# Folded weight chunks whose accumulating transfer begins ahead of their cast, transposes one step later, and one folded pair more in each down block

## The chip, the core and the metric

The kernel runs on one core of a Trainium2 chip. The time is the device time of one execution in microseconds (us), as the median of several executions. Beside it there is one profiled execution, from which all views of the trace come; its time is a little above the median of the others.

## The reference

One decoder layer in float32, with 256 tokens (`x` is 1 x 256 x 2048): a first feed-forward block, two token mixers side by side (retention and sliding-window attention), a second feed-forward block and a gated per-layer embedding, each followed by a layer norm. The two feed-forward blocks take most of the time, and the change lies in them:

```python
D_MODEL, SEQ, D_FF = 2048, 256, 5632
def swiglu(x, w_gu, w_down):
    g, u = jnp.split(x @ w_gu, 2, axis=-1)
    return (jax.nn.silu(g) * u) @ w_down
...
h = layer_norm(alpha * h + 0.5 * swiglu(h, w_ffn1_gu[i], w_ffn1_down[i]), ln_g[i, 0], ln_b[i, 0])
...
h = layer_norm(alpha * h + mixed, ln_g[i, 1], ln_b[i, 1])
h = layer_norm(alpha * h + 0.5 * swiglu(h, w_ffn2_gu[i], w_ffn2_down[i]), ln_g[i, 2], ln_b[i, 2])
```

## The kernel before

**Products in three matmuls.** The matmuls run on fp32r data. A float32 operand is split in a high part (a rounding copy on ACT, line 105) and a low part (the rest, a subtraction on DVE, line 106), and a product is three matmuls: low by high, high by high, high by low (`Sum.add`, lines 431 to 433). The activations are the stationary operand, the weights move: each matmul is 128 x 128 by 128 x 512.

**Chunks and slots.** Weights come from memory in chunks of 128 x 1024 words (512 KB), by transfers on SP's queue (line 119 and its neighbours: `Chunk`). A chunk's raw, high and low form take one slot each of a pool of 46 slots (`SLOTS`), which the weights share with other buffers; `slots_for_weights(n)` says how many of them the weights may use from that point on.

**Units.** The rows of a weight matrix are taken in pairs of 128-row blocks, and the columns in two halves. A pair is one unit of a block's order string: `P` is plain, two `Single` chunks of 12 matmuls each. `S` is a `Seven`: four quarter products by seven multiplications instead of eight (21 matmuls instead of 24), for which DVE first adds raw quarters to each other (lines 226 to 229) and two more forms, u and v, are split. `D` is a `Seven` of the second feed-forward block whose forms were prepared ahead of it and are only loaded. `F` is *folded*: a `Single`, and then a `Folded` chunk, whose low part DVE does not make. ACT writes minus the raw data, rounded (line 169), POOL issues a transfer inside the chip's memory that adds the raw data to it (line 170), and ACT makes the high part by a rounding copy (line 171).

**Two matrices.** In the first feed-forward block (names with f1) the gate and up products run in 11 groups `j` of 512 columns each: group 0 is all `P`, the others have the order "FFSSFSSP" (three `F`, four `S`, one `P`). In the second (f2), groups 1 to 3 have no `F`, groups 4 to 7 one, group 8 two, 9 and 10 three. After a group's last `S`, `seven_common` combines the sums (lines 549 to 553: one copy on ACT, then additions on DVE into tiles `eve` and `evw`), the Silu follows on ACT (line 1057), and the result is transposed: a `Turn` copies halves of words on ACT (line 185), SP moves them by a transposing transfer (line 189), ACT joins them again (line 196). The down product has two halves of the columns, with the orders FIRST_DOWN and SECOND_DOWN over 22 pairs; the tile names are f1d, f1e (or f2d, f2e) for its sums.

**What sets the order.** The program text is generated in the order in which the engines run it, and `plan` is a list of units in the order of use. `fill` moves units on: it loads the next of the plan while fewer than `far` matmuls' worth of units are waiting and slots are left, and it lets ACT, DVE and POOL make the next loaded unit while less than `ahead` (45) matmuls' worth of them is ready. Each unit says how many slots its load takes (`loads`), how many its making needs (`makes`) and how many it holds until its use (`keeps`), and its matmuls (`time`). `take` gives the next ready unit to PE, `done` frees its slots and calls `fill`. After each unit `run_side` does one waiting side job: `later(n, job)` puts a job n steps on. A transpose is such a job: its transfer is issued DELAY steps after its copies, and the join three steps after that (`turned`, lines 984 to 995). SP's, POOL's and each engine's instructions run in order: one that waits holds all behind it.

Of the kernel before, what the change touches and what calls it, by code (L numbers as in the profile page):

```python
# [9 lines left out]
F32R = mybir.dt.float32r  # L10
# [28 lines left out]
SLOTS = 46  # L39


SEVEN = (0, 1, 2, 3)

AHEAD = {1: (4, 5), 2: (4,), 3: (4, 5), 4: (4,), 5: (4, 5), 6: (4,), 7: (4, 5)}
AHEAD_SLOTS = 36

DELAY = 1

SEVEN_DOWN = (6, 7, 8, 9)

FIRST_DOWN = "PPPPPPFFSFSPSFSPSFSSPS"
SECOND_DOWN = "PPPSPSPSFSPSFSSPSPPPPP"
LEAD = 4

# [8 lines left out]
def layer(ctx: ExitStack, tc: tile.TileContext, io):  # L63
# [16 lines left out]
    def slot(shape, dt, name):  # L80
        return slots.tile(shape, dt, tag="slot", name=name)
# [6 lines left out]
    plan = []  # L88
# [19 lines left out]
    class Chunk:  # L108
# [31 lines left out]
    class Single:  # L140


        loads, makes, keeps, time = 1, 2, 2, 12
# [4 lines left out]
        def load(self, **how):  # L148
            self.chunk = Chunk(self.key, **how)
# [1 line left out]
        def make(self):  # L151
            self.chunk.make()

    class Folded:

        loads, makes, keeps, time = 1, 2, 2, 12

        def __init__(self, key):  # L160
            self.key = key

        def load(self, **how):
            self.chunk = Chunk(self.key, **how)

        def make(self):
            c = self.chunk
            c.make_hi()
            act.mul(c.lo, c.raw, -1.0)
            pool.dma_start(c.lo, c.raw, accum_op=ALU.add)  # L170
            act.copy(c.hi, c.raw)

    class Turn:

# [138 lines left out]
    loaded, ready = [], []  # L313
    room = {"slots": 0, "used": 0, "ahead": 45, "far": 90, "quiet": False}

    def fill(must=False):

        while True:
            queued = sum(u.time for u in ready)
            left = room["slots"] - room["used"]  # L320
            wanted = must and not ready or not room["quiet"] and queued < room["ahead"]
            if loaded and wanted and loaded[0].makes <= left:
                u = loaded.pop(0)
                u.make()
                room["used"] += u.keeps - u.loads
                ready.append(u)
                continue
            first = loaded[0] if loaded else plan[0] if plan else None
            queued += sum(u.time for u in loaded)
            if plan and queued < room["far"] and plan[0].loads + first.makes <= left:  # L330
                u = plan.pop(0)
                u.load()
                room["used"] += u.loads
                loaded.append(u)
                continue
            return

    def make_next():
        u = loaded.pop(0)
        assert u.makes <= room["slots"] - room["used"]  # L340
        u.make()
        room["used"] += u.keeps - u.loads
        ready.append(u)

    def take(key):
        if not ready:
            fill(True)
        u = ready.pop(0)
        assert u.key == key, (u.key, key)
        return u  # L350
# [5 lines left out]
    def slots_for_weights(n, ahead=45, far=90):  # L356
        room.update(slots=n, ahead=ahead, far=far)
# [95 lines left out]
    def block_units(units, keys):  # L453

        for kind, p in units:
            if kind == "P":
                plan.extend(Single(keys(n, p)) for n in range(2))
            elif kind == "F":
                plan.extend(of(keys(n, p)) for n, of in enumerate((Single, Folded)))
            else:  # L460
                plan.append((Seven if kind == "S" else Prepared)(keys(0, p), keys(1, p)))

# [511 lines left out]
    def ffn(name, i, ht, norm, keep, residual, keepers, away):  # L974
# [33 lines left out]
        for j in range(KF // 4):  # L1008
            pg, pu = banks(f"{name}g{j}"), banks(f"{name}u{j}")
            units = gu_units(name, j)  # L1010
            n_of = {(0, 0): KD, (0, 1): KD, (1, 0): KD, (1, 1): KD}
            for kind, p in units:
                if kind in "SD":
                    for at in ((0, 0), (0, 1), (1, 0)):
                        n_of[at] -= 1
                    n_of[1, 1] -= 2
            sums = [[Sum((pg, pu)[n][t], n_of[t, n]) for n in range(2)] for t in range(2)]
            got = []

            if norm is not None and j == 0:  # L1020
                front, units = units[:FRONT_PAIRS], units[FRONT_PAIRS:]
                steps = [(gu_keys(name, 0)(n, p), 2 * p, n) for _, p in front for n in range(2)]
                norm.by_transfer = 3,
                norm.first(steps, rhs, sums, (
                    (3, (1, 0)), (5, "more"), (5, (1, 1)), (7, (0, 2)), (8, (1, 2)), (9, (0, 3)), (9, (1, 3)),
                    (10, ("move", 3)), (10, "go"),
                ))
                later(1, lambda: norm.join(3))
                slots_for_weights(24)

            def before(u, j=j, offset=KD // 2 - len(units)):
                u += offset
                if j == 0 and norm is None and u % 2 == 0:
                    first_chunk(u // 2)
                    if u == 6:
                        slots_for_weights(24)
                    if u == 2:
                        load_constants()
                if j == 0 and u == 7:
                    for g in sorted({p // 2 for p in SEVEN}):  # L1040
                        hi, lo = (slot([P, 8, P], F32R, f"{name}f{w}{g}") for w in "hl")
                        made[g] = seven_forms(keep[g], hi, lo)
                    if name == "f2":
                        g = AHEAD[1][0] // 2
                        made[g] = forms_of([ht[:, 4 * g : 4 * g + 4, :]], f"{name}f{g}")
                if name == "f2" and j and u == 0:
                    slots_for_weights(AHEAD_SLOTS - j)
                if j == KF // 4 - 1 and u in (4, 6):
                    convert(u // 2 - 2)

            block(f"{name}{j}", units, gu_keys(name, j), rhs, forms, sums, lambda *a: got.extend(seven_common(*a)), before)
            if got:
                g, v = got
                for x, ps in ((g, pg), (v, pu)):
                    for t in range(2):
                        dve.tensor_tensor(x[:, t], x[:, t], ps[t], ALU.add)  # L1056
                act.activation(g, g, AF.Silu)  # L1057
                dve.tensor_tensor(v, g, v, ALU.mult)
            else:
                v = slot([P, 2, 512], F32, f"{name}v{j}")  # L1060
                for t in range(2):
                    act.activation(v[:, t], pg[t], AF.Silu)
                for t in range(2):
                    dve.tensor_tensor(v[:, t], v[:, t], pu[t], ALU.mult)
            later(1, lambda j=j, v=v: turned(j, v))
# [878 lines left out]
```

## Time and profile before

| what | us |
|---|---|
| time, median of 3 runs (2226.49 to 2227.42) | 2227.09 |
| the profiled execution's own time | 2230.62 |
| its span in the trace | 2228.6 |
| busy: PE / DVE / ACT / POOL | 2218.5 / 2004.0 / 1439.0 / 50.9 |
| gate and up of the first block, groups 1 to 10 | about 49 to 458 |
| its down product, first and second half | about 458 to 581, 581 to 689 |
| mixers, and the start of the second block | about 689 to 1495 |
| gate and up of the second block, groups 1 to 10 | about 1495 to 1895 |
| its down product, first half | about 1895 to 2018 |

The clock that TensorE was granted is 0.999 of full speed over the span. In the rows of the timeline the first figure is the start in us from the span's start, the second the duration, then engine, line, operation, output<-inputs, and in brackets the idle time of the engine just before and what ended it. Matmuls are pipelined: a row shows 0.39 us for one, while the next begins 0.23 us after it.

### The profile page before, as it was taken

How to read it: one execution, taken by the hardware profiler on the slowest of the kernel's cores; microseconds unless marked ns; L12 is line 12 of the kernel's file. 1: busy time of each engine (PE TensorE's matmuls, PEld its weight loads, DVE VectorE, ACT ScalarE, POOL GpSimd, SP SyncE). 2: the span in 40 equal slices, each digit the busy share in tenths (PEclk: the TensorE clock that was granted, in tenths of full speed). 3: DMA queues.
4: the chain of work that ended last, by engine and by line, in shares of the span. 5: the costliest groups of instructions: out<-in, count | busy, mean ns of one | idle time of the engine just before them, and what ended most of it. 6: DMA issues, size and time to landing. Idle time of an engine off the chain costs nothing.

```text
span 2228.6 us, 29103 instructions
## 1 busy us (share of the span) xinstructions
PE 2218.5 (100%) x10140; PEld 1838.9 (83%) x10140; DVE 2004.0 (90%) x2624; ACT 1439.0 (65%) x1677; POOL 50.9 (2%) x65
## 2 busy tenths in 40 slices
PE   9999999999999999999999999999999999999998
PEld 8888888888888888888788888888888888888887
DVE  6999999989998789789999888779999999999977
ACT  6777777777565545557865567466766677765653
POOL 0000000000000000000000000000000000000000
PEclk9999999999999999999999999999999999999999
DMA  9988998976686889757976568888999999666871
GB/s 321 250 264 252 249 263 241 269 227 217 228 305 234 298 283 338 203 179 232 291 233 226 184 203 321 316 302 266 301 301 295 300 248 276 209 233 221 309 283 68
DMA packets 302075, 570.51 MB, mean 256 GB/s; under 512 B 98652, under 2 KB 103388, under 8 KB 301928
## 3 DMA queue, kind: packets, MB, share of 16 engines
q1 hardware_dynamic: 291880, 536.71, 72.3%
q0 software_dynamic: 8064, 29.36, 7.0%
q10 hardware_dynamic: 1984, 2.58, 0.4%
q8 instruction: 79, 1.29, 0.2%
q14 instruction: 68, 0.56, 0.1%
HBM read 487.32 MB, written 31.46 MB: 233 GB/s over the span
## 4 chain that ended last, share of the span: by engine, by line
PE 93%; DMA 3%; DVE 2%; issue 1%; ACT 0%; SPq 0%; ACTq 0%; POOL 0%; DVEq 0%; POOLq 0%
PE rqk L382 3%; PE f2g L431 3%; PE f2g L433 3%; PE f2g L432 3%; PE f1g L431 2%; PE f1g L433 2%; PE f1g L432 2%; PE f2u L431 2%; PE f2u L433 2%; PE f2u L432 2%; PE f1u L433 2%; PE f1u L431 2%; PE f1u L432 2%; PE aqk L382 2%; PE f2e L431 1%; PE f1e L431 1%
## 5 line engine op out<-in xcount | busy, mean ns | idle before, releaser
L106 DVE TENSOR_TENSOR lf_gu<-rf_gu,hf_gu 128x1024 fp32r<-128x1024 f32 (+1 forms) x225 | 267.7, 1210 | 22.1 <-ACT hf_gu L105 21.1
L105 ACT CAST hf_gu<-rf_gu 128x1024 fp32r<-128x1024 f32 (+1 forms) x225 | 228.7, 1039 | 22.1 <-DMA rf_gu<-in_f_gu 21.5
L106 DVE TENSOR_TENSOR lw_in_f<-rw_in_f,hw_in_f 128x1024 fp32r<-128x1024 f32 x140 | 167.8, 1219 | 15.0 <-ACT hw_in_f L105 15.0
L106 DVE TENSOR_TENSOR lf_down<-rf_down,hf_down 128x1024 fp32r<-128x1024 f32 x130 | 155.7, 1220 | 12.9 <-ACT hf_down L105 11.1
L105 ACT CAST huf_gu<-uf_gu 128x1024 fp32r<-128x1024 f32 x76 | 80.1, 1053 | 125.4 <-DVE uf_gu L227 109.4
L105 ACT CAST hf_down<-rf_down 128x1024 fp32r<-128x1024 f32 x130 | 132.7, 1049 | 30.5 <-DMA rf_down<-in_f_down 21.3
L105 ACT CAST hw_in_f<-rw_in_f 128x1024 fp32r<-128x1024 f32 x140 | 140.4, 1049 | 2.3 <-PE gt L433 1.6
L105 ACT CAST hvf_gu<-vf_gu 128x1024 fp32r<-128x1024 f32 x76 | 80.1, 1054 | 32.4 <-DVE vf_gu L229 30.5
L106 DVE TENSOR_TENSOR luf_gu<-uf_gu,huf_gu 128x1024 fp32r<-128x1024 f32 x76 | 92.6, 1218 | 0.0
L106 DVE TENSOR_TENSOR lvf_gu<-vf_gu,hvf_gu 128x1024 fp32r<-128x1024 f32 x76 | 92.6, 1218 | 0.0
L431 PE MATMUL f1g<-hf_gu,xt 128*128 128x512 f32 x232 | 90.8, 391 | 0.0
L433 PE MATMUL f1g<-lf_gu,xt 128*128 128x512 f32 x232 | 90.5, 390 | 0.0
L432 PE MATMUL f1g<-hf_gu,xt 128*128 128x512 f32 x232 | 90.5, 390 | 0.0
L431 PE MATMUL f2g<-hf_gu,ht 128*128 128x512 f32 x211 | 82.2, 390 | 0.0
L433 PE MATMUL f2g<-lf_gu,ht 128*128 128x512 f32 x211 | 82.1, 389 | 0.0
L432 PE MATMUL f2g<-hf_gu,ht 128*128 128x512 f32 x211 | 82.1, 389 | 0.0
L433 PE MATMUL f1u<-lf_gu,xt 128*128 128x512 f32 x192 | 75.0, 391 | 1.2 <-DMA lf_gu<-rf_gu 1.2
L431 PE MATMUL f1u<-hf_gu,xt 128*128 128x512 f32 x192 | 74.7, 389 | 0.0
L432 PE MATMUL f1u<-hf_gu,xt 128*128 128x512 f32 x192 | 74.7, 389 | 0.0
L170 POOL DMA_DIRECT2D lf_gu<-rf_gu x42 | 36.4, 867 | 1641.2 <-DMA rf_gu<-in_f_gu 1017.6
L105 ACT CAST huf_down<-uf_down 128x1024 fp32r<-128x1024 f32 x32 | 33.7, 1054 | 60.7 <-DVE uf_down L227 58.7
L1057 ACT ACTIVATE eve<-eve 128x1024 f32<-128x1024 f32 x20 | 21.2, 1061 | 67.3 <-DVE eve L1056 67.3
(1512 smaller groups left out, 6978.3 us busy)
## 6 DMA issues: line engine op xcount, KB each, us to landing
rf_gu<-in_f_gu SPq DMA_DIRECT2D x361, 512.0 KB
rf_down<-in_f_down SPq DMA_DIRECT2D x176, 512.0 KB
rw_in_f<-in_w_in_f SPq DMA_DIRECT2D x148, 512.0 KB
lf_gu<-rf_gu POOLq DMA_DIRECT2D x42, 512.0 KB, 8.2
rw_rv<-in_w_rv SPq DMA_DIRECT2D x32, 512.0 KB
rw_ret<-in_w_ret SPq DMA_DIRECT2D x32, 512.0 KB
rw_mix<-in_w_mix SPq DMA_DIRECT2D x32, 512.0 KB
rw_pg<-in_w_pg SPq DMA_DIRECT2D x32, 512.0 KB
```

The source lines that it names most:

```text
L105: act.copy(dst_hi, src)
L106: (lo_engine or dve).tensor_tensor(dst_lo, src, dst_hi, ALU.subtract)
L170: pool.dma_start(c.lo, c.raw, accum_op=ALU.add)
L382: pe.matmul(ps[f], hi[:, kk, f * P : (f + 1) * P], rhs(k), start=k == 0, stop=k == n_k - 1,)
L431: pe.matmul(o, al, bh, start=first, stop=False)
L432: pe.matmul(o, ah, bh, start=False, stop=False)
L433: pe.matmul(o, ah, bl, start=False, stop=self.left == 0)
L1057: act.activation(g, g, AF.Silu)
```

## The change

Four edits. **First**, a folded chunk becomes two entries of the plan. `Folding` loads the raw data, and its making is the multiplication on ACT and POOL's accumulating transfer; it has no matmuls (`time` 0) and never comes to `ready`. `Folded` stands where it stood, loads nothing and makes the high part alone. `fold_at` puts the `Folding` 34 matmuls' worth of units ahead (12 in the down product), and if a `Seven` stands within the entries just before that place, ahead of that `Seven`. `take` calls `fill` until something is ready. **Second**, DELAY is 2 instead of 1: a transpose's transfer and its join come one side step later. **Third**, FIRST_DOWN has one `F` more and one `P` less, and its last two adjoining `S` are apart. **Fourth**, in group 0 of the first block the weights get 30 slots instead of 24 from the seventh unit on. The matmuls are the same in number and kind.

```diff
+FOLD_AHEAD = 12, 34
...
-DELAY = 1
+DELAY = 2
...
-FIRST_DOWN = "PPPPPPFFSFSPSFSPSFSSPS"
+FIRST_DOWN = "PPPPPFFSFSFSPSFSPSFSPS"
...
-    class Folded:
-        loads, makes, keeps, time = 1, 2, 2, 12
+    class Folding:
+        loads, makes, keeps, time = 1, 1, 2, 0
...
-        def load(self, **how):
-            self.chunk = Chunk(self.key, **how)
+        def load(self):
+            self.chunk = Chunk(self.key)

         def make(self):
             c = self.chunk
-            c.make_hi()
+            c.lo = slot(list(c.raw.shape), F32R, "l" + c.name)
             act.mul(c.lo, c.raw, -1.0)
             pool.dma_start(c.lo, c.raw, accum_op=ALU.add)
+
+    class Folded:
+        loads, makes, keeps, time = 0, 1, 2, 12
...
+        def make(self):
+            c = self.chunk = self.begun.chunk
+            c.hi = slot(list(c.raw.shape), F32R, "h" + c.name)
             act.copy(c.hi, c.raw)
+            room["used"] -= self.begun.keeps
+
+    def fold_at(ahead, key):
+        begun = Folding(key)
+        at, time = len(plan), 0
+        while at > 0 and time < ahead:
+            at -= 1
+            time += plan[at].time
+        if ahead and any(isinstance(u, Seven) for u in plan[at - 12 : at + 1]):
+            while not isinstance(plan[at], Seven):
+                at -= 1
+        plan.insert(at, begun)
+        plan.append(Folded(begun))
...
-        ready.append(u)
+        if u.time:
+            ready.append(u)
...
-        if not ready:
+        while not ready:
             fill(True)
...
-                plan.extend(of(keys(n, p)) for n, of in enumerate((Single, Folded)))
+                plan.append(Single(keys(0, p)))
+                fold_at(FOLD_AHEAD[keys(1, p)[0][-3:] == "_gu"], keys(1, p))
...
-                        slots_for_weights(24)
+                        slots_for_weights(30)
```

What moves is shown at three places. In the names r, h, l stand for raw, high and low, u and v (with h and l before them) for the two forms of a `Seven` and b for its fourth operand; the two numbers behind gu are the half of the columns and the pair, the last is a running number; the new lines are numbered some 2 (casts) to 30 higher.

ACT in the first block, from the second-last `S` of group 4 (pair 2) on, first before:

```order
L105 CAST huf_gu_0_2_1759<-uf_gu_0_2_1746 128x1024
L105 CAST hvf_gu_0_2_1763<-vf_gu_0_2_1747 128x1024
L105 CAST hf_gu_0_3_1787<-rf_gu_0_3_1691 128x1024
L105 CAST bf_gu_0_3_1791<-rf_gu_1_3_1693 128x512
L105 CAST huf_gu_0_3_1794<-uf_gu_0_3_1781 128x1024
L105 CAST hvf_gu_0_3_1798<-vf_gu_0_3_1782 128x1024
L196 COPY f1a_1804<-mf_1695 128x2x4x128 x2
L105 CAST hf_gu_0_7_1819<-rf_gu_0_7_1723 128x1024
L105 CAST hf_gu_1_7_1846<-rf_gu_1_7_1767 128x1024
L105 CAST hf_gu_0_4_1875<-rf_gu_0_4_1802 128x1024
L169 ACTIVATE lf_gu_1_4_1880<-rf_gu_1_4_1823 128x1024
L171 CAST hf_gu_1_4_1879<-rf_gu_1_4_1823 128x1024
```

and now:

```order
L107 CAST huf_gu_0_2_1763<-uf_gu_0_2_1750 128x1024
L107 CAST hvf_gu_0_2_1767<-vf_gu_0_2_1751 128x1024
L170 ACTIVATE lf_gu_1_4_1785<-rf_gu_1_4_1694 128x1024
L170 ACTIVATE lf_gu_1_5_1788<-rf_gu_1_5_1696 128x1024
L107 CAST hf_gu_0_3_1797<-rf_gu_0_3_1698 128x1024
L107 CAST bf_gu_0_3_1801<-rf_gu_1_3_1700 128x512
L107 CAST huf_gu_0_3_1804<-uf_gu_0_3_1791 128x1024
L107 CAST hvf_gu_0_3_1808<-vf_gu_0_3_1792 128x1024
L107 CAST hf_gu_0_7_1826<-rf_gu_0_7_1725 128x1024
L226 COPY f1a_1830<-mf_1727 128x2x4x128 x2
L107 CAST hf_gu_1_7_1854<-rf_gu_1_7_1771 128x1024
L107 CAST hf_gu_0_4_1881<-rf_gu_0_4_1812 128x1024
```

The multiplications of the next group's folded chunks 4 and 5 stand ahead of the last `S` (pair 3) instead of behind it, with the high part's cast left at its place, and the join `f1a` comes one cast later.

ACT at the end of the same group, from the Silu on, before:

```order
L1057 ACTIVATE eve<-eve 128x1024
L105 CAST hf_gu_0_0_1964<-rf_gu_0_0_1884 128x1024
L105 CAST bf_gu_0_0_1968<-rf_gu_1_0_1886 128x512
L105 CAST huf_gu_0_0_1971<-uf_gu_0_0_1958 128x1024
L105 CAST hvf_gu_0_0_1975<-vf_gu_0_0_1959 128x1024
L185 COPY wf_1995<-evw 128x1024 x2
L105 CAST hf_gu_0_1_2016<-rf_gu_0_1_1911 128x1024
L105 CAST bf_gu_0_1_2020<-rf_gu_1_1_1913 128x512
L105 CAST huf_gu_0_1_2023<-uf_gu_0_1_2010 128x1024
L105 CAST hvf_gu_0_1_2027<-vf_gu_0_1_2011 128x1024
L105 CAST hf_gu_0_6_2047<-rf_gu_0_6_1979 128x1024
L169 ACTIVATE lf_gu_1_6_2079<-rf_gu_1_6_1993 128x1024
```

and now:

```order
L1086 ACTIVATE eve<-eve 128x1024
L170 ACTIVATE lf_gu_1_6_1960<-rf_gu_1_6_1887 128x1024
L107 CAST hf_gu_0_0_1969<-rf_gu_0_0_1889 128x1024
L107 CAST bf_gu_0_0_1973<-rf_gu_1_0_1891 128x512
L107 CAST huf_gu_0_0_1976<-uf_gu_0_0_1963 128x1024
L107 CAST hvf_gu_0_0_1980<-vf_gu_0_0_1964 128x1024
L215 COPY wf_1998<-evw 128x1024 x2
```

Chunk 6's multiplication follows the Silu directly instead of standing eleven rows behind it.

SP's queue at the end of the first half of the down product, with the last pairs' raw chunks, before:

```order
L119 DMA rf_down_20_4717<-in_f_down 128x1024
L119 DMA rf_down_20_4777<-in_f_down 128x1024
L119 DMA rf_down_17_4779<-in_f_down 128x1024
L119 DMA rf_down_17_4781<-in_f_down 128x1024
L119 DMA rf_down_18_4803<-in_f_down 128x1024
L119 DMA rf_down_18_4805<-in_f_down 128x1024
L119 DMA rf_down_21_4911<-in_f_down 128x1024
L119 DMA rf_down_21_4938<-in_f_down 128x1024
L119 DMA rf_down_19_4965<-in_f_down 128x1024
L119 DMA rf_down_19_4967<-in_f_down 128x1024
L119 DMA rf_down_0_4990<-in_f_down 128x1024
L119 DMA rf_down_0_4992<-in_f_down 128x1024
```

and now:

```order
L121 DMA rf_down_20_4740<-in_f_down 128x1024
L121 DMA rf_down_17_4742<-in_f_down 128x1024
L121 DMA rf_down_17_4744<-in_f_down 128x1024
L121 DMA rf_down_20_4766<-in_f_down 128x1024
L121 DMA rf_down_18_4833<-in_f_down 128x1024
L121 DMA rf_down_18_4835<-in_f_down 128x1024
L121 DMA rf_down_21_4853<-in_f_down 128x1024
L121 DMA rf_down_21_4911<-in_f_down 128x1024
L121 DMA rf_down_19_4913<-in_f_down 128x1024
L121 DMA rf_down_19_4915<-in_f_down 128x1024
L121 DMA rf_down_0_4933<-in_f_down 128x1024
L121 DMA rf_down_0_4993<-in_f_down 128x1024
```

The rows stand in nearly the same order on this queue, but they wait for slots that other units free: the matmul that frees a slot for pair 19's second chunk stands 18 places earlier among PE's matmuls than before, in both feed-forward blocks, and the first use of pair 19 stands at the same place.

More of the change, by code (lines that the diff above doesn't have):

```diff
@@ L152, in make, with __init__, load @@
             self.chunk.make()
-    class Folded:
-        loads, makes, keeps, time = 1, 2, 2, 12
+    class Folding:
+        loads, makes, keeps, time = 1, 1, 2, 0
         def __init__(self, key):
             self.key = key
-        def load(self, **how):
-            self.chunk = Chunk(self.key, **how)
+        def load(self):
+            self.chunk = Chunk(self.key)
         def make(self):
             c = self.chunk
-            c.make_hi()
+            c.lo = slot(list(c.raw.shape), F32R, "l" + c.name)
             act.mul(c.lo, c.raw, -1.0)
             pool.dma_start(c.lo, c.raw, accum_op=ALU.add)
-            act.copy(c.hi, c.raw)
+    class Folded:
+        loads, makes, keeps, time = 0, 1, 2, 12
+        def __init__(self, begun):
+            self.key, self.begun = begun.key, begun
+        def load(self):
+            pass
+        def make(self):
+            c = self.chunk = self.begun.chunk
+            c.hi = slot(list(c.raw.shape), F32R, "h" + c.name)
+            act.copy(c.hi, c.raw)
+            room["used"] -= self.begun.keeps
[10 more added lines that the diff above has]
+        plan.append(Folded(begun))
     class Turn:
@@ L322, in fill @@
             if loaded and wanted and loaded[0].makes <= left:
-                u = loaded.pop(0)
-                u.make()
-                room["used"] += u.keeps - u.loads
-                ready.append(u)
+                make_next()
                 continue
@@ L342, in make_next @@
         room["used"] += u.keeps - u.loads
-        ready.append(u)
+        if u.time:
+            ready.append(u)
     def take(key):
-        if not ready:
+        while not ready:
             fill(True)
```

## The prediction

> **What bounds the kernel now.** I read the busy table of the page first, then the waits of PE, then the timeline of PE around each wait, then the engines that released it.
>
> ```profile
> PE 2218.5 (100%) x10140; PEld 1838.9 (83%) x10140; DVE 2004.0 (90%) x2624; ACT 1439.0 (65%) x1677; POOL 50.9 (2%) x65
> ```
>
> PE is busy for 2218.5 of 2228.6 us. The change leaves the matmuls as they are, so it can only alter the time in which PE stands still. The waits of PE say how little that is (engine, line, releaser: total, times, longest):
>
> ```profile
> PE warm L1822 <- POOL ident masks.py:199: 1.4, 1, 1.4
> PE f1u L433 <- DMA lf_gu<-rf_gu: 1.2, 2, 0.9
> PE f1e L431 <- DVE evw L550: 0.6, 1, 0.6
> PE mr1a L433 <- DVE lw_ret L106: 0.5, 1, 0.5
> PE f2e L431 <- DVE evw L550: 0.5, 1, 0.5
> ...
> PE mr1s L433 <- DVE lvw_ret L106: 0.2, 1, 0.2
> ```
>
> The change speaks to the second, third and fifth row. The first is the start, the others lie in the mixers. These figures are too small, because a matmul's shown end (0.39 us after its start) overlaps the next start. The true loss is read from start to start. In steady work starts are 0.2267 us apart; around the waits of f1u:
>
> ```profile
> 74.70 0.50 PE L433 MATMUL f1u<-lf_gu,xt 128*128 128x512 f32 x1 [0.88 <-DMA lf_gu<-rf_gu]
> ...
> 237.81 0.39 PE L432 MATMUL f1u<-hf_gu,xt 128*128 128x512 f32 x1
> 238.54 0.50 PE L433 MATMUL f1u<-lf_gu,xt 128*128 128x512 f32 x1 [0.34 <-DMA lf_gu<-rf_gu]
> 238.88 0.39 PE L431 MATMUL f1u<-hf_gu,xt 128*128 128x512 f32 x1
> ...
> 401.65 0.39 PE L432 MATMUL f1u<-hf_gu,xt 128*128 128x512 f32 x1
> 401.96 0.50 PE L433 MATMUL f1u<-lf_gu,xt 128*128 128x512 f32 x1
> ```
>
> At 238.54 the start is 0.73 us after the one before, 0.50 more than the step, and the next is 0.34 later, 0.11 more than the step: 0.61 us lost where the row says 0.34 idle, so 0.27 is to be added to an idle figure. At 74.70 that makes 0.88 + 0.27 = 1.15. At 401.96 no idle is shown, yet 0.31 − 0.23 + 0.11 = 0.19 is lost. **Together 1.95 us for f1u.**
>
> **Why f1u waits.** The low part of a folded chunk is a multiplication by −1 on ACT (L169) and an accumulating transfer issued by POOL (L170):
>
> ```profile
> 62.38 1.06 ACT L169 ACTIVATE lf_gu<-rf_gu 128x1024 fp32r<-128x1024 f32 x1
> ...
> 63.73 0.86 POOL L170 DMA_DIRECT2D lf_gu<-rf_gu  x1 [15.21 <-ACT lf_gu L169]
> ...
> lf_gu<-rf_gu POOLq DMA_DIRECT2D x1, 512.0 KB, 10.9
> ...
> 228.02 1.06 ACT L169 ACTIVATE lf_gu<-rf_gu 128x1024 fp32r<-128x1024 f32 x1
> ...
> 229.58 0.86 POOL L170 DMA_DIRECT2D lf_gu<-rf_gu  x1 [17.85 <-ACT lf_gu L169]
> ...
> q0 software_dynamic: 144, 0.52, 22.0%
> ...
> lf_gu<-rf_gu POOLq DMA_DIRECT2D x1, 512.0 KB, 8.9
> ```
>
> The last figures of the two "POOLq" rows are the us from issue to landing, from the DMA view of 62 to 75 and of 228 to 240; the q0 row is from the latter. 63.73 + 10.9 = 74.63 and 229.58 + 8.9 = 238.48: in both cases PE goes 0.06 to 0.07 us after the landing. From the start of the multiplication to the landing it is 12.25 and 10.46 us, the longest such stretches I found, and both belong to the third folded chunk of a group (chunk 6).
>
> **Part 1, the earlier accumulation.** In a group of f1 chunk 6's multiplication now follows the Silu (L1057 in the old numbering) directly, and those of chunks 4 and 5 stand ahead of the last seven's first cast. Old rows at these two places, and the first uses of the low parts that the second place serves:
>
> ```profile
> 214.14 1.06 ACT L1057 ACTIVATE eve<-eve 128x1024 f32<-128x1024 f32 x1 [2.69 <-DVE eve L1056]
> 215.11 1.04 ACT L105 CAST hf_gu<-rf_gu 128x1024 fp32r<-128x1024 f32 x1
> ...
> 217.98 1.05 ACT L105 CAST huf_gu<-uf_gu 128x1024 fp32r<-128x1024 f32 x1 [1.32 <-DVE uf_gu L227]
> ...
> 234.91 1.05 ACT L105 CAST hf_gu<-rf_gu 128x1024 fp32r<-128x1024 f32 x1
> ...
> 239.17 1.06 ACT L105 CAST huf_gu<-uf_gu 128x1024 fp32r<-128x1024 f32 x1 [2.69 <-DVE uf_gu L227]
> ...
> 259.08 0.39 PE L433 MATMUL f1u<-lf_gu,xt 128*128 128x512 f32 x1
> ```
>
> Chunk 6 would be multiplied at 215.1 and is wanted at 238.04 (237.81 + 0.23): 22.9 us, against 12.25 needed at worst. The other two start at 234.9 for 259.08, 24 us. Even a landing 10 us later than any seen would do, so I take the whole 1.95. At 74.70 the multiplication moves ten instructions forward on ACT, each 0.97 us from start to start where nothing is waited for (214.14 to 215.11), so some 9.7 us where 1.15 is missing. From below the gain is 0, if what delays the landing moves with it.
>
> What ACT pays: the multiplication takes the same 0.97 us. After the Silu one is put in, and the 1.32 us that ACT stood idle ahead of huf cover it. Ahead of the last seven two are put in, 1.94 us, and the 2.69 us before huf at 239.17 cover them. With no cover DVE, which waits for these casts, would be up to 1.94 us later per group. Later on ACT the same multiplications are gone, so nothing is added over a group.
>
> **Part 2, the down block.** One pair there turns from plain into folded: per block one multiplication more on ACT (1.06), one subtraction less on DVE (1.2), one issue more on POOL (0.86). None of these is on PE's path. What counts is the order at the end of the first half:
>
> ```profile
> 558.00 5.72 DMA rf_down<-in_f_down
> ...
> 558.19 2.35 DVE L106 TENSOR_TENSOR lf_down<-rf_down,hf_down 128x1024 fp32r<-128x1024 f32 x2
> 563.84 0.69 DVE L226 TENSOR_TENSOR uf_down<-rf_down,rf_down 128x512 f32<-128x512 f32 x1 [3.29 <-DMA rf_down<-in_f_down]
> ...
> 575.05 0.68 DVE L550 TENSOR_TENSOR evw<-eve,f1d0s 128x512 f32<-128x512 f32 x1
> ...
> 572.51 0.59 ACT L549 COPY eve<-f1d0s 128x512 f32<-128x512 f32 x1 [0.71 <-PE f1d0s L433]
> ...
> 574.81 0.39 PE L433 MATMUL f1e<-lf_down,f1ah 128*128 128x512 f32 x1
> 575.79 0.50 PE L431 MATMUL f1e<-hf_down,f1al 128*128 128x512 f32 x1 [0.59 <-DVE evw L550]
> ...
> 2012.27 0.39 PE L433 MATMUL f2e<-lf_down,f2ah 128*128 128x512 f32 x1
> 2013.18 0.50 PE L431 MATMUL f2e<-hf_down,f2al 128*128 128x512 f32 x1 [0.52 <-DVE evw L550]
> ```
>
> The chain of waits shows that the last seven's raw chunk (pair 19) starts to load when PE frees a slot at 558.00 and lands at 563.72. DVE, done at 560.54 with what it had (558.19 + 2.35), stands still until 563.84, works through without a gap and reaches evw at 575.05. PE wants the bank that evw reads at 575.04 and gets it at 575.79. In the new order the slot of pair 19 is freed by a matmul that stands 18 places earlier among PE's: 18 × 0.2267 = 4.1 us, so the chunk lands at 559.6, and DVE's start is set by 560.54: 3.3 us sooner. Then DVE is ready for evw at 571.75, and the copy that evw also needs ends at 572.51 + 0.59 = 573.10; evw runs from 573.1 to 573.8, 1.2 us ahead of PE. ACT's copy itself waits for PE (0.71, released by PE), so it doesn't move. The loss at 575.79 is 0.59 + 0.27 = 0.86 and at 2013.18, where the same order runs again, 0.52 + 0.27 = 0.79. **Together 1.65 us.** From below 0, if pair 19 lands no sooner.
>
> **Part 3, the rest, at nothing.** Transposes one step later on SP free that queue of waits for ACT, and the copies that join a transposed group come after one more of the casts that DVE uses. DVE gets more lead, PE nothing. The 30 slots at the start of f1 touch a stretch where PE never stands still, so there is nothing to win, and at most a wait to lose:
>
> ```profile
> 6.00:49.00 43.00, 43.00 (x188) 35.02 (x187) 31.38 (x34) 28.89 (x31) 1.87 (x2) 1.00 1.00 343
> 49.00:458.00 409.00, 407.78 (x1797) 336.77 (x1796) 384.27 (x457) 305.20 (x330) 24.15 (x28) 1.00 0.92 257
> ```
>
> (Columns: window, length, busy of PE, its loads, DVE, ACT, POOL, clock, DMA share, GB/s.) The DMA share is 1.00 there: moving loads can't speed them, and the chunks moved ahead by one or two places push others by about 512 KB / 343 GB/s = 1.5 us each.
>
> **Sum.** 1.95 + 1.65 = 3.6 us. The profiled execution took 2230.62, so the same execution would take 2227.0; the median of the runs is 3.53 lower at 2227.09, and I set the change off against it: **2223.5 us**, 0.16% less. A difference under 0.2%, 4.45 us, counts as no change in this measurement.
>
> **The rivals.** First, *slower, because accumulations now run where the last seven's raw chunks are loading.* In f1 the DMA share is 0.92, and one accumulation took 22.0% of the engines for 12 us, 2.64 us of all sixteen. In the second FFN loads already come last at this place:
>
> ```profile
> 1718.07 0.62 ACT L105 CAST bf_gu<-rf_gu 128x512 fp32r<-128x512 f32 x1 [0.60 <-DMA rf_gu<-in_f_gu]
> ...
> 1724.90 1.22 DVE L106 TENSOR_TENSOR lvf_gu<-vf_gu,hvf_gu 128x1024 fp32r<-128x1024 f32 x1
> ...
> 1726.67 0.39 PE L433 MATMUL f26s<-lvf_gu,f2fh 128*128 128x512 f32 x1
> ```
>
> ACT waits 0.60 for the chunk, and the low part that follows is done at 1726.12 for a matmul at 1726.67: 0.55 us of lead. If the chunk landed 2.64 us later, PE would lose 2.09 in such a group. Seven groups of the second FFN (4 to 10) hold a folded chunk: up to 14.6 us, 2223.5 + 14.6 = 2238.1; it decides from about four such groups (8.4 − 3.6 = 4.8 us slower). Against it: the accumulation was there before too, only later in the group, and transposes leave the stretch. The Trainium skill speaks for it ("DMA: Bandwidth & Descriptors", section "SWDGE vs HWDGE vs iDMA"): transfers issued by GpSimd and by SP feed different queues inside the same engines, which alternate between them. By that rule an accumulation takes its turns from the loads beside it, and the sum would be the 2238.1 above; the trace agrees as to the sharing, with 22.0% for the one queue while loads go on.
>
> Second, *only one of the parts works.* If landings follow the clock of something else and not the issue, f1u stays: 2227.09 − 1.65 = 2225.4. If pair 19 lands no sooner, or ACT's copy takes the place of DVE as the last, f1e and f2e stay: 2227.09 − 1.95 = 2225.1. For it: small waits often get a successor. Against it: 10 us and 1.2 us of room.
>
> Third, *more goes than was counted.* The two waits in the mixers (0.5 and 0.2 shown, 0.27 to be added to each, 1.24) could shift with everything ahead of them: 2223.5 − 1.2 = 2222.3, just over the 0.2%. Nothing in the change touches them, but the phase of the transfers does.
>
> Fourth, *nothing changes*, 2227.1: the waits removed appear at the next matmul that is as late. Against it: PE's next waits were listed, and there are none between.
>
> **The numbers.** The forecast (2222.7 to 2224.6) 0.56; one part only 0.14; nothing 0.04; more than counted 0.13; slower 0.13. Faster by over 0.2% (below 2222.64): 0.14. Slower (above 2231.54): 0.12, the slower rival but for its mild end. Same: 0.74. For 8 times in 10 the range runs from 2221.9 to 2226.8: forecast, one part, and most of the third rival.
>
> **What would show it.** Right: no idle on f1u from an accumulation, landings over 8 us ahead of their use; pair 19 landing before 560.6 and DVE's gap of 3.3 us gone; evw done before PE wants its bank; no wait of ACT for raw chunks in f1 and none longer than the 0.60 above at the last sevens of the second FFN. Wrong: waits of PE for lvf or lf from DVE in the last seven of a group; ACT waiting at a multiplication for its chunk; a wait of PE in the first 50 us. A time over 2227 would mean that a step of part 1 or 2 failed, and over 2231.5 that loads or ACT are late in many groups.

## The result, and the profile after

The changed kernel takes 2247.12 us (median of 5, 2245.22 to 2251.30), the kernel before 2227.42 (median of 5 runs with it): 19.7 us slower, a ratio of 1.0092 with a 95% interval of 1.0077 to 1.0106. The forecast was 2223.5. The profiled execution took the 2247.12 us itself, with a span of 2245.3; before, it was 2230.62.

The busy table of the page and PE's waits (engine, line, releaser: total, times, longest) of the changed kernel:

```profile
PE 2220.4 (99%) x10140; PEld 1839.3 (82%) x10140; DVE 2000.8 (89%) x2622; ACT 1440.8 (64%) x1679; POOL 52.7 (2%) x67
...
PE f2u L459 <- ACT hf_gu L107: 13.3, 1, 13.3
PE f28s L461 <- DVE lf_gu L108: 1.6, 1, 1.6
PE warm L1851 <- POOL ident masks.py:199: 1.4, 1, 1.4
PE f26s L461 <- DVE luf_gu L108: 0.8, 1, 0.8
PE f2g L459 <- DVE evw L579: 0.6, 1, 0.6
```

The waits that the forecast counted, f1u, f1e and f2e, are not in the list any more. In their place stands one wait of 13.3 us in the second feed-forward block, and smaller ones near it. Where the time went can be read from the same matmuls in both traces. First the kernel before, then the changed one: the first matmul of a seven in f1, the first of its down product, and the same two of f2.

```profile
60.97 0.39 PE L431 MATMUL f11s<-hf_gu,xt 128*128 128x512 f32 x1
...
460.11 0.39 PE L431 MATMUL f1d<-hf_down,f1al 128*128 128x512 f32 x1
...
1505.22 0.39 PE L431 MATMUL f21s<-hf_gu,ht 128*128 128x512 f32 x1
...
1897.58 0.39 PE L431 MATMUL f2d<-hf_down,f2al 128*128 128x512 f32 x1
```

```profile
60.78 0.39 PE L459 MATMUL f11s<-hf_gu,xt 128*128 128x512 f32 x1
...
457.90 0.39 PE L459 MATMUL f1d<-hf_down,f1al 128*128 128x512 f32 x1
...
1501.00 0.39 PE L459 MATMUL f21s<-hf_gu,ht 128*128 128x512 f32 x1
...
1914.94 0.39 PE L459 MATMUL f2d<-hf_down,f2al 128*128 128x512 f32 x1
```

Gate and up of f1 took 399.14 us and now take 397.12: 2.0 us gained. From there to f2 it was 1045.11 and is 1043.10: 2.0 us gained, 0.9 in the down block and the rest in the mixers. Gate and up of f2 took 392.36 and now take 413.94: **21.6 us lost in that one stage.** Its window says the same (length, busy of PE, PE's loads, DVE, ACT, POOL, clock, DMA share, GB/s), first before, then after; then the 26 us around the long wait:

```profile
1495.00:1895.00 400.00, 400.00 (x1766) 331.22 (x1765) 381.51 (x451) 281.69 (x309) 10.38 (x12) 1.00 0.92 285
```

```profile
1495.00:1895.00 400.00, 382.95 (x1672) 313.44 (x1670) 360.00 (x430) 264.07 (x290) 10.38 (x12) 0.98 0.93 266
...
1757.00:1783.00 26.00, 13.26 (x59) 10.66 (x57) 7.82 (x9) 4.35 (x5) 0.00 (x0) 0.81 1.22 103
```

PE, DVE and ACT all stand still for most of those 26 us. The DMA share is above 1 (it adds up the packets' times, which overlap), and yet only 103 GB/s are moved, where the kernel before moved 285 over the same stage. So the transfers hold up everything. The timeline shows which; SP's queue, POOL, ACT and PE of the changed kernel:

```profile
1749.80 9.60 SPq L219 DMA_TRANSPOSE mf<-wf  x1
...
1752.43 0.86 POOL L171 DMA_DIRECT2D lf_gu<-rf_gu  x1 [35.77 <-ACT lf_gu L170]
...
1782.44 1.04 ACT L107 CAST hf_gu<-rf_gu 128x1024 fp32r<-128x1024 f32 x1 [19.48 <-DMA rf_gu<-in_f_gu]
...
1783.54 0.80 PE L459 MATMUL f2u<-hf_gu,ht 128*128 128x512 f32 x1 [13.28 <-ACT hf_gu L107]
...
1785.39 0.63 PE L459 MATMUL f2u<-hf_gu,ht 128*128 128x512 f32 x1
1785.82 0.63 PE L460 MATMUL f2u<-hf_gu,ht 128*128 128x512 f32 x1
```

A transposing transfer (group 6's result) is issued at 1749.80 and, while SP is still at it, an accumulating one (group 8's first folded chunk) at 1752.43. The DMA view of 1758 to 1779 us in the changed kernel, with packets, their sizes, and the time of each queue's packets as a share of the sixteen engines:

```profile
DMA packets 1824, 1.06 MB, mean 50 GB/s; under 512 B 1632, under 2 KB 1632, under 8 KB 1823
...
q1 hardware_dynamic: 1689, 0.55, 99.6%
q0 software_dynamic: 134, 0.49, 28.5%
```

A transpose consists of 2048 packets of 256 bytes on SP's queue q1; an accumulation is 128 packets of 4 KB and 16 short ones on POOL's queue q0. In 21 us 1632 packets of the transpose went, 78 per us. The same group's transpose in the kernel before, in a window of 5 us:

```profile
DMA packets 2196, 0.92 MB, mean 184 GB/s; under 512 B 2100, under 2 KB 2100, under 8 KB 2196
```

There no accumulation is in flight, and by its packets the transpose took 3.85 us; in the changed kernel it took 24.9 (1754.5 to 1779.4). The weight load that ACT waits for stands behind the transpose on SP's queue; it is issued at 1759.51 and takes 22.85 us (from the chain of waits):

```profile
1759.51 22.85 DMA rf_gu<-in_f_gu
```

In the changed kernel a second transpose, that of group 4, overlaps an accumulation at its end only (221 packets left) and takes 7.2 us.

### The profile page after: what moved, and what is told of

Read it like the earlier page. It is cut to its first block, busy times and chain, and to the rows that moved or that the text cites. A ratio compares the mean times of both kernels' runs of the same rounds, so it can differ in the third digit from the quotient of the medians.

```text
span 2245.3 us, 29156 instructions
## 1 busy us (share of the span) xinstructions
PE 2220.4 (99%) x10140; PEld 1839.3 (82%) x10140; DVE 2000.8 (89%) x2622; ACT 1440.8 (64%) x1679; POOL 52.7 (2%) x67
## 4 chain that ended last, share of the span: by engine, by line
PE 92%; DVE 4%; DMA 2%; issue 1%; ACT 0%; SPq 0%; ACTq 0%; DVEq 0%
PE f1g L461 3%; PE f1g L459 3%; PE f1g L460 3%; PE rqk L410 3%; PE f1u L460 2%; PE f1u L461 2%; PE f1u L459 2%; PE f2g L459 2%; PE f2g L461 2%; PE f2g L460 2%; DMA rf_gu<-in_f_gu 2%; PE f2u L459 2%; PE f2u L460 2%; PE f2u L461 2%; PE aqk L410 2%; PE f2e L459 1%
## 5 line engine op out<-in xcount | busy, mean ns | idle before, releaser
L459 PE MATMUL f2u<-hf_gu,ht 128*128 128x512 f32 x164 | 64.8, 395 | 13.3 <-ACT hf_gu L107 13.3
```

Source lines behind the costliest of these rows:

```text
L459: pe.matmul(o, al, bh, start=first, stop=False)
```

## The experiments

Theory T: the overlap of a transpose with an accumulation in flight is the loss. Rival L: the loads come late because the folded chunks' raw data now goes ahead of the last sevens'. All runs below but the two of transfers alone were timed beside the kernel before on their own chip, where it took 2228.8 us; ratios are to that.

### DELAY back at 1

```diff
-DELAY = 2
+DELAY = 1
```

> The changed kernel with DELAY back at 1 and everything else of the change kept. Theory T (a transposing transfer and an accumulating one that are in flight together slow each other about tenfold; in the changed kernel this hits at 1754 to 1779 us): every transpose goes one step sooner, the one of 1754.5 is through before the accumulation's first packet at 1757.8, no transpose takes over 6 us, and the gains of the forecast come through: 2223 to 2226 us. Rival L (the folded chunks' raw data now load ahead of the last seven's and push those back, and SP's queue is blocked behind them): the order of the loads is the same as in the changed kernel, so the stall of 13 us stays: 2238 to 2247 us.

Measured: 2226.37 us, ratio 0.9989 (0.9980 to 0.9999). No transpose overlaps an accumulation, the longest of the feed-forward blocks takes 6.1 us, and PE's waits for f1u from an accumulation, f1e and f2e are gone. This is 0.4 us above T's range and 12 below L's, with the order of the weight loads as in the changed kernel; it doesn't tell yet whether the transposes' place or the overlap is the cause. This version is 20.8 us under the changed kernel, and 2.4 us under the kernel before, which is only just clear of the noise.

### DELAY 2 alone

```diff
-DELAY = 1
+DELAY = 2
```

The edit is to the kernel before.

> The kernel before with DELAY 2 and nothing else of the change. Theory T: transposes move by 3 to 5 us; those of 266.98, 391.54, 433.31 and 1829.19, 1870.84 us then come to lie beside accumulations that are in flight in the kernel before at 273.8 to 277.7, 397.2 to 401.4, 436.2 to 439.7, 1834.5 to 1838.7 and 1873.4 to 1878.1 us: at least one transpose of over 6 us with a stall of PE behind it where the two overlap, 2230 to 2260 us. Rival L: a change of DELAY alone moves no weight load ahead of another, 2226 to 2229 us.

Measured: 2232.17 us (2225.70 to 2242.80 in ten runs), ratio 1.0019 (1.0004 to 1.0034). Of the five transposes that T named, two overlap an accumulation in the trace, with 321 and 361 packets left, and take 7.4 and 8.8 us; the second makes PE wait:

```profile
PE f2u L433 <- DMA lf_gu<-rf_gu: 4.5, 1, 4.5
```

L has no room for that. The spread is what an overlap that is sometimes hit and sometimes missed would give; only one of the ten runs has a trace, so this is not shown.

### No lead in the second block's gate and up

```diff
-                fold_at(FOLD_AHEAD[keys(1, p)[0][-3:] == "_gu"], keys(1, p))
+                fold_at(0 if keys(1, p)[0] == "f2_gu" else FOLD_AHEAD[...], keys(1, p))
```

> The changed kernel, but in the second feed-forward block's gate and up the folded chunks begin where they began before (ahead 0); DELAY stays 2. Rival L: no raw chunk is loaded ahead of a last seven there, the stalls of 1716 to 1819 us go, and the rest of the change gains its 3.6 us: 2223 to 2226 us. Theory T: the collision at 1754 goes (accumulations lay at 1732 to 1740 there), but the transposes, a step later than before, come beside the old accumulations of the groups 8 to 10 (1793 to 1797, 1834 to 1839, 1873 to 1878 us): again a transpose of over 6 us where two overlap, 2228 to 2260 us.

Measured: 2226.02 us, ratio 0.9995 (0.9984 to 1.0005), with two of ten runs at 2231.49 and 2236.10. In the profiled execution (2225.68 us) three accumulations begin beside a transpose when some 10, 29 and 111 of its packets are left, and the transpose ends within 0.3 us. T's range was missed by 2 us, L's met to within 0.02; this run alone would speak for L.

### FIRST_DOWN alone

```diff
-FIRST_DOWN = "PPPPPPFFSFSPSFSPSFSSPS"
+FIRST_DOWN = "PPPPPFFSFSFSPSFSPSFSPS"
```

The edit is to the kernel before.

> The kernel before with the new FIRST_DOWN and nothing else of the change. Both theories, as the forecast's part 2: the waits for evw at 575.8 and 2013.2 us go, 0.86 + 0.79 us, so 2225 to 2226 us, and nothing else moves. If pair 19 lands no sooner, 2227.

Measured: 2234.25 us, ratio 1.0025 (1.0015 to 1.0036): slower, where both theories said 1.6 us faster. PE's waits in this kernel:

```profile
PE f1d L433 <- DMA lf_down<-rf_down: 3.3, 1, 3.3
...
PE f2d L433 <- DMA lf_down<-rf_down: 1.3, 1, 1.3
```

The waits for evw are gone as forecast, but the order brings a folded chunk's use so near to its accumulation that PE waits for it in both blocks. From start to start PE loses 5.1 us there in the first block, of which 1.7 are slower matmuls behind the wait, and 1.6 in the second. Less the 1.65 us saved that makes 5.1 us, and the spans of the two traces differ by 5.0.

### Moving another transpose

```diff
-            later(DELAY, turn.move)
-            later(DELAY + 3, joined)
+            delay = 1 if name == "f2" and j == 7 else DELAY
+            later(delay, turn.move)
+            later(delay + 3, joined)
```

> The changed kernel with one transpose alone, that of group 7 of the second feed-forward block, issued one step sooner again; nothing else differs. Theory T (the collision of this one transpose with the accumulation for group 8 is the loss): the long transpose and the stall of 13.4 us behind it go, with the slow matmuls that follow it, about 16 us: 2226 to 2232 us. Rival L (loads that come late since folded raw data goes ahead of them): the loads keep their order but for this transpose, the stall stays within a few us: 2240 to 2247.

> The other way round: the changed kernel with DELAY 1, which took 2226.4 us, and the transpose of group 7 of the second feed-forward block alone at DELAY 2. Theory T: the collision comes back by itself, a transpose of 15 to 25 us with 1000 packets or more left when the accumulation begins, and 2236 to 2247 us. Rival (it takes all the later transposes together): 2226 to 2229 us.

Both named the wrong transpose: the transposes follow their groups, and the one that collided at 1754 us is group 6's. So both missed T's range, and they show what moving a transpose that doesn't collide does: nothing. The first took 2248.49 us, with the same long overlap (1585 packets left, 21.4 us) and another (873 left, 13.8 us). The second, the mirrored edit on DELAY 1, took 2227.27 us, ratio 0.9992 (0.9982 to 1.0001), with no overlap.

### DELAY 2 in the first block, 1 in the second

```diff
+            delay = 1 if name == "f2" else DELAY
```

> A version meant to win: the changed kernel with DELAY 2 in the first feed-forward block, where the changed kernel showed no collision, and 1 in the second. Theory T: no transpose overlaps an accumulation, and the waits of f1u, f1e and f2e stay away: 2222 to 2226 us. Rival (late transposes cost something else in the first block): not below 2226.4, the time with DELAY 1 everywhere.

Measured: 2226.82 us, ratio 0.9992 (0.9983 to 1.0001). No overlap. Its median is above the 2226 of T's range, and not below DELAY 1 everywhere.

### The two transposes that collided

```diff
+            delay = 1 if name == "f2" and j in (4, 6) else DELAY
```

> The changed kernel with two transposes one step sooner, those of the groups 4 and 6 of the second feed-forward block; these are the ones that collided in the changed kernel (1670 and 1754 us), while the run before this moved the transpose of group 7, which did not collide. Theory T (the accumulation that is in flight beside the transpose is the loss): neither transpose overlaps an accumulation, the stall of 13.4 us and those of 1 to 2 us near it go, 2225 to 2230 us. Rival L (loads late on SP's queue because folded raw data goes ahead): 2240 to 2250 us.

Measured: 2226.58 us, ratio 0.9991 (0.9981 to 1.0001). Of 41 transposes two are issued sooner, and 20 us are back. Group 6's transpose and group 8's first accumulation no longer meet:

```profile
1742.80 4.70 SPq L219 DMA_TRANSPOSE mf<-wf  x1
...
1753.22 0.86 POOL L171 DMA_DIRECT2D lf_gu<-rf_gu  x1 [37.49 <-ACT lf_gu L170]
```

By its packets the transpose takes 3.6 us, from 1745.45 on. The other way round, DELAY 1 with these two at 2:

> The changed kernel with DELAY 1 everywhere (2226.4 us) but for the same two transposes, which have DELAY 2. Theory T: at least one of them comes to overlap an accumulation again, with a transpose of over 7 us; if it is the one of group 6 with 1000 packets or more left, 2238 to 2250 us, if only a few hundred are left, 2228 to 2232 us. Rival L: 2225 to 2229 us, since the loads keep their order.

Measured: 2242.02 us, ratio 1.0060 (1.0041 to 1.0079). Group 6's transpose overlaps an accumulation with 1070 packets left and takes 14.2 us, group 4's with 261 left and 6.9. L expected 2225 to 2229.

### Two accumulations left out

```diff
-            pool.dma_start(c.lo, c.raw, accum_op=ALU.add)
+            if self.key not in (("f2_gu", 6, 1, 6), ("f2_gu", 8, 1, 5)):
+                pool.dma_start(c.lo, c.raw, accum_op=ALU.add)
```

> The changed kernel without two of its 58 accumulating transfers, those beside the two slow transposes (group 6's and the first of group 8's folded chunks of the second feed-forward block); their low parts then hold minus the raw data, so that part of the sum is not computed, while all casts, multiplications, loads, transposes and matmuls stay as they are. Theory T: without the accumulation the two transposes take 3 to 6 us and the stalls go: 2224 to 2230 us. Rival L, and any theory by which the transposes' later place on SP's queue is the loss by itself: 2240 to 2250 us.

Measured: 2226.45 us, ratio 0.9992 (0.9983 to 1.0001). The transposes and loads keep their late places on SP's queue, and the loss is gone. The DMA view of 1752 to 1758 us:

```profile
DMA packets 2534, 1.41 MB, mean 235 GB/s; under 512 B 2109, under 2 KB 2109, under 8 KB 2533
...
q1 hardware_dynamic: 2533, 1.39, 110.4%
```

No packet of an accumulation (q0) is there any more, and group 6's transpose takes 4.7 us beside loads on its own queue. This settles T against L, and against the later place by itself.

### The down block's part alone

```diff
-FOLD_AHEAD = 12, 34
+FOLD_AHEAD = 12, 0
-DELAY = 2
+DELAY = 1
-                        slots_for_weights(30)
+                        slots_for_weights(24)
```

> Only the down block's part of the change: the new FIRST_DOWN with accumulations 12 matmuls' worth ahead in the down blocks, and DELAY 1, 24 slots and no lead in gate and up as before. With the order alone the time was 5.5 us above that of the kernel before, with waits of 3.3 and 1.3 us for an accumulation in the down blocks. If those came from its late start, they go here, and so do the waits for evw (0.86 + 0.79 us): 1 to 2.5 us under the kernel before. If the new order is slow for another reason: 3 to 6 us over it.

Measured: 2228.21 us, ratio 0.9996 (0.9986 to 1.0005). In the trace PE waits neither for an accumulation nor for evw in the down blocks, while one wait for f1u is left. So the lead of 12 takes away the 5.5 us that the order alone costs. The 1 to 2.5 us under the kernel before that were expected did not show: 0.6 us less is not told from no change.

### Transfers alone

The first of two kernels of transfers alone:

> A small kernel of transfers alone, which leaves the whole computation out and writes zeros: a transpose alone, an accumulation alone, an accumulation with a transpose triggered 0, 1 and 2 ACT copies (0.95 us each) behind it, a transpose with the accumulation triggered right behind it, a copying transfer by POOL that does not accumulate with a transpose 1 copy behind it, and an accumulation beside three weight loads; all of it twice. Theory T: a transpose alone takes 2.6 us and an accumulation 4.2 us; where the accumulation goes first, the transpose's packets that are left at its first packet go at about 75 per us instead of about 800, so up to 27 us for both; where the transpose goes first, the accumulation starts only when the transpose is nearly through, and neither is slow. If it is the accumulating that matters, the copying transfer leaves the transpose at 2.6 to 4 us; if any transfer issued by POOL does it, it is slow there as well. Beside loads the accumulation stays under 9 us. Rival (the slowness needs the other traffic of the full kernel): none of the transposes takes over 6 us.

By its packets a transpose alone took 2.6 us both times, an accumulation alone 4.7 us from issue to landing. With the two triggered together, the transpose took 9.2 us (676 packets left when the accumulation began) and 6.1 us (356 left), though nothing else was moving. The DMA view of the first:

```profile
DMA packets 2190, 1.02 MB, mean 110 GB/s; under 512 B 2069, under 2 KB 2069, under 8 KB 2190
...
q0 software_dynamic: 128, 0.50, 62.2%
q1 hardware_dynamic: 2062, 0.52, 43.6%
```

With one or two copies between the triggers the accumulation was almost through, and the transpose took 2.7 and 2.6 us. With the transpose first, the accumulation began when 134 and 150 packets were left, and the transpose took 3.2 us. The copying transfer by POOL was all but over when its transpose began (0.3 us of overlap), and the accumulation meant to run beside three loads was issued 27 us after the last of their packets. So the questions of the copy and of the loads stayed open.

> A second small kernel of transfers alone (the computation is left out, zeros are written): beside a transpose, one other transfer of 512 KB of four kinds: accumulating by POOL from on-chip memory, copying by POOL from on-chip memory, a weight load issued by POOL, a weight load issued by ACT. Each with 0, 2, 4 and 6 small ACT copies between the two triggers, the other transfer first. If the accumulating is what slows the transpose, only the first kind shows transposes of over 5 us, where the two overlap with some hundred transpose packets left, and the others stay at 2.6 to 5 us. If any transfer issued by POOL does it, the first three kinds show it and the load by ACT does not. If any transfer of another queue does it, all four do.

Transposes beside an accumulation took 5.1 and 5.0 us with gaps of 0 and 2 (overlapped), 2.6 with gaps of 4 and 6 (no overlap worth the name). With gap 0 the accumulation began when 207 packets were left; with gap 2 it began 0.3 us ahead of the transpose, and took 3.3 us by its packets, as with gaps of 4 and 6. Beside a copy by POOL with gap 0, which also began first, it was 3.9 us. Beside a weight load issued by POOL with gap 0 the transpose took 6.7 us, with 1601 packets left when the load began:

```profile
q1 hardware_dynamic: 2080, 0.52, 67.8%
q0 software_dynamic: 144, 0.52, 28.0%
...
l<-in_f_gu POOLq DMA_DIRECT2D x1, 512.0 KB, 7.4
m<-w SPq DMA_TRANSPOSE x1, 8.4
```

The loads issued by ACT all began ahead of the transpose and overlapped it for 1 us at most. So it isn't the accumulating alone: a load by POOL that begins in the middle slows a transpose too, but less. The 1601 packets took 6.0 us, where the 1595 of the changed kernel took 21.6 (there beside other loads). Whether a load by ACT would is not shown.

## Why the prediction was wrong

**Part 1 was right.** Its place on ACT in the changed kernel, group 4's end:

```profile
211.38 1.06 ACT L1086 ACTIVATE eve<-eve 128x1024 f32<-128x1024 f32 x1 [3.30 <-DVE eve L1085]
212.35 1.04 ACT L170 ACTIVATE lf_gu<-rf_gu 128x1024 fp32r<-128x1024 f32 x1
...
216.61 1.06 ACT L107 CAST huf_gu<-uf_gu 128x1024 fp32r<-128x1024 f32 x1 [1.76 <-DVE uf_gu L257]
```

The multiplication follows the Silu and ACT still waits 1.76 us for DVE behind it, so it was covered. f1u's waits went: gate and up of f1 gained 2.0 us where 1.95 was forecast, and in the trace no matmul there starts more than 0.23 us after the one before.

**Part 2 was right in the whole, and wrong on one price.** DVE starts pair 19 without its stall of 3.3 us, and PE no longer waits for evw, in the changed kernel:

```profile
557.15 0.69 DVE L256 TENSOR_TENSOR uf_down<-rf_down,rf_down 128x512 f32<-128x512 f32 x1 [0.24 <-PE f1d L460]
...
570.94 0.68 DVE L579 TENSOR_TENSOR evw<-eve,f1d0s 128x512 f32<-128x512 f32 x1
```

But it priced the one folded pair more at its work on ACT, DVE and POOL, none of it on PE's path, and not at its accumulation's landing. Alone that costs 5.5 us; part 1's lead of 12 pays it back, as the run of the down block alone shows.

**Part 3 failed.** "Transposes one step later on SP free that queue of waits for ACT ... DVE gets more lead, PE nothing" was the wrong step: it put the later transposes at nothing for PE, and beside part 1's earlier accumulations they cost 21.6 us in one stage. Issuing two of them one step sooner gives 20 us back. It looked at the transposes as places on SP's queue and on ACT, and not as 2048 packets that are in flight for 3 us beside whatever POOL has started. Part 1 likewise looked at the accumulations' landing times against their use, and not at what they would now lie beside. Each of these two edits by itself is harmless or nearly so (leads with DELAY 1: 2226.37; DELAY 2 alone: 2232.17); the two together let an accumulation begin while a transpose has 1595 of its 2048 packets to go. The 30 slots, which part 3 also put at nothing, were not tried alone.

**The sign came, its reading did not hold.** PE's waits for `lf` and `lvf` from DVE in sevens of the second block (1.6 and 0.2 us at the longest) come near one of the signs that the prediction named, and it read a time over 2231.5 as loads or ACT late in many groups. It was one transfer: 13.3 us at one matmul, and small waits in the groups beside it.

**The first rival came out on the right side for another reason.** It had the place (the second block, accumulations in the way of raw chunks) and the sharing of the engines, but expected 2.64 us per group in seven groups, from how long an accumulation occupies the engines. What decided is one long overlap. And its argument against, "transposes leave the stretch", was the reverse of what happened. The Trainium skill's rule of queues that alternate ("DMA: Bandwidth & Descriptors", section "SWDGE vs HWDGE vs iDMA") fits a part of it. In the second kernel of transfers alone, a transpose that began beside a running accumulation (gap 2) got 112 packets started while the accumulation started 112, one for one, in 2.3 us (49 per us); after the last 4 KB packet it went at 716 per us. But taking turns would end with the accumulation, which takes 2.8 to 5.6 us everywhere else in the two kernels. That the accumulation itself then needed 23 us is not explained by it, and nothing here shows what holds both back.

**The second and fourth rivals** did not occur. Of the third, the mixers did get a little shorter (by 1.1 us in the profiled execution) where nothing in the change touches them; in the run with DELAY 1 they took longer than before instead.

In sum: the forecast terms came to 3.6 us and were there, in 2.0 + 0.9 + 0.8 us of shorter stages; the profiled execution is 16.5 us longer because the second block's gate and up lost 21.6.

## What to carry to other kernels

A transfer that is moved has to be checked against the transfers that it will then run beside, not only against the instructions that wait for it; in this kernel a transposing transfer was a bad neighbour for one that POOL started a moment later. Two edits that each move transfers by a few us are tried apart before they go together. A version whose runs spread over more than 10 us where others spread over 3 may have a collision that it hits now and then; here that is argued from the spread alone. An order that puts a new user behind a slow producer is only as good as the lead that the producer gets.

## What the runs showed of the hardware

In the runs of the kernel with a trace the price of an overlap goes with the packets left in the transpose when the accumulation's first packet comes. Counted from the packets in the traces (to within some five), 221 left took 2.8 us from then on, 261 took 2.9, 321 took 4.3, 361 took 5.4, 873 took 10.4, 1070 took 12.2, 1585 took 18.7 and 1595 took 21.6. That is 67 to 91 packets per us, against 2048 in 2.6 us alone, near 790 per us: about a tenth. The fall is sharp: in the run with two transposes moved later, group 6's got 489 packets started in the half us before the accumulation's first, 237 in the half us after it, and then 9 and 7. How many are left depends also on the loads ahead on the same queue: in the changed kernel 257 load packets started among the transpose's first 453, in 3.2 us. With 111 left or fewer the transpose ended within 0.3 us.

Mostly the overlap did not come about: where POOL issued an accumulation after the transpose's first packet, its own first packet came when the transpose had 10 to 60 packets left, or none. In the slow cases of the kernel POOL issued 2 to 3 us after SP began the transpose (0.1 us in the two kernels of transfers alone), and ahead of its first packet. That is no sharp rule: two accumulations issued ahead of that first packet by 0.8 and 0.1 us found 111 and 41 packets left. And where the accumulation was already running when the transpose began (gap 2 above), neither crawled.

After the long wait the matmuls ran slower for a while, 0.43 us from start to start instead of 0.23 (1785.39 to 1785.82 in the changed kernel), with a granted clock of 0.84 in the 12 us from 1783 on and of 0.81 in the window of the wait. From 1783.54 to 1787.41 that adds up to 1.8 us more than at the usual step. So the wait of 13.3 us cost PE some 2 us more than its own length.
